# Prologue of a one-layer Hyena encoder: a new order of work, a shorter sine argument and transposes that nobody reads

## The chip, the cores and the metric

One NeuronCore of a Trainium2 chip runs the kernel. The metric is the device time of one execution in microseconds (us); less is better. The core has a matrix engine (PE), a vector engine (DVE), an activation engine (ACT), a general engine (POOL) and a synchronization engine (SP). Each works through its own queue in order. DMA transfers are started from the queues of SP, ACT and POOL and run beside the engines. PE writes only to PSUM, a small memory of eight banks; the other data lie in SBUF.

## What is computed

One Hyena layer followed by a SwiGLU channel mixer, on 1024 tokens of 1024 channels in float32. Cut to what matters here:

```python
def hyena_filter(L, w1, b1, w2, b2, w3, b3, freq, w_out, decay):
    ...
    act = lambda a: jnp.sin(fr * a)
    h = act(feat @ w1.astype(f32) + b1.astype(f32))
    h = act(h @ w2.astype(f32) + b2.astype(f32))
    h = act(h @ w3.astype(f32) + b3.astype(f32))
    h = (h @ w_out.astype(f32)).reshape(L, 2, D_MODEL)
    h = h * jnp.exp(-t[:, :, None] * jnp.abs(decay.astype(f32)))
    ...

def hyena_mixer(u, ...):
    z = short_conv(u @ w_in + b_in, conv_w, conv_b)      # width 3 along the tokens
    x0, x1, v = jnp.split(z, 3, axis=-1)
    s = (v * x1).astype(jnp.float32)
    g = hyena_filter(...)
    y = irfft(rfft(s, n=2L) * rfft(g, n=2L))[:, :L]
    y = (y + s * skip) * x0
    return y @ w_out + b_out

def reference(...):
    h = rmsnorm(x, norm_mix[i])
    x = x + hyena_mixer(h, ...)
    x = x + swiglu(rmsnorm(x, norm_ffn[i]), ...)
    return rmsnorm(x, norm_final)
```

The prologue is everything up to the first filter: the first RMS norm, its transposition, the first projections of `u @ w_in`, and the three sine layers of the filter.

## The kernel before, in words

**Numbers and tiles.** The 1024 tokens form 8 tiles of 128 (`xs[0..7]`), each with all 1024 channels. A float32 product is made from two parts of each operand: a high part, rounded to a shorter format, and a low part, the rest. Three of the four products of parts are summed (`TERMS`): high by high, high weight by low activation, low weight by high activation. One block of weights is `w_in[:, n*128:(n+1)*128]`; it gives `z{n}`, 128 channels by 1024 tokens, in two PSUM banks. Blocks 16 to 23 belong to `v`, 8 to 15 to `x1`, 0 to 7 to `x0`.

**Normalizing and turning.** For each tile ACT sums the squares (`square`, L269), ACT and DVE make the reciprocal root (`rstd`, L178 to L183), DVE multiplies by it and by the norm weight `gmix` (`scaled`, L280), PE transposes the tile with an identity matrix (`turn_in`, L285), ACT writes the high part (`u_high`, L292) and DVE the low part (`u_low`, L295). Tiles 4 and 5, and 6 and 7, share one `rstd`; tiles 0 to 3 have one each. `gmix` is loaded by SP with the same 4 KB row sent to all 128 partitions.

**Weights.** SP loads a block (`w_load`), ACT writes its high part (`w_high`, L199) and minus the high part into the place of the low part (L157), and a DMA of POOL's queue adds the raw block to that (L158). The raw tile can take the next block only after this DMA has landed.

**The sine layers.** PE multiplies (`mlp_mm`, L313), DVE adds the bias, multiplies by the frequency and takes off a multiple of two pi in eight passes of 512 elements (`mlp_angle`, L323 to L332), ACT takes the sine (`mlp_sin`, L335). After the third, `both_mm` (L340) and `hs_parts` (L346, L347) give the operand `hs` of the filter's product.

**The filter's window.** `F_[0].ready` and `F_[0].window(j)` take eight exponentials on ACT (L492). `taps` (L518, L519) multiplies the filter's product by them on DVE.

**The short convolution.** For `v` (`v_conv`) ACT makes the middle tap and both side taps, and two DMAs of POOL's queue add the side taps (L406, L416). For `x1` DVE adds them in four passes (`conv_rest`, L384, L385).

**Order.** The whole Hyena part is under a manual schedule: the order in which the program issues work is the order in each engine's queue, SP's and POOL's among them. After the prologue come eight periods, one for each 128 channels. A period begins with `taps_mm` (L511, L512), the first two steps of the next projection, and `spectrum_mm` (L528, L529). In the FFN behind, a planner sets the order of PE, DVE, ACT and POOL from estimated times.

**PSUM.** There are two slots of two banks with the tag `mm` and two with the tag `cv`. Before, all transposed tiles go through `cv`, and `mm` holds `z16` and `z8`. A slot is free again when the last reader or writer of its tile has finished.

Of the kernel before, what the change touches and what calls it, by code (L numbers as in the profile page):

```python
# [110 lines left out]
def hyena_ffn_kernel(ctx: ExitStack, tc: tile.TileContext, a: dict, out: bass.AP):  # L111
# [61 lines left out]
    S.sqrt(warm, ones)

    def rstd_of(ss, n, nm):
        w = small(nm, 4 * n, tag=f"rs{n}", bufs=2)
        sc, rt, r0, q = (w[:, i * n : (i + 1) * n] for i in range(4))
        V.tensor_scalar(sc, ss, 1.0 / D, EPS, ALU.mult, ALU.add)  # L178
        S.sqrt(rt, sc)
        V.reciprocal(r0, rt)  # L180
        V.scalar_tensor_tensor(q, sc, -0.5, r0, ALU.mult, ALU.mult)
        V.tensor_tensor(q, q, r0, ALU.mult)
        V.scalar_tensor_tensor(r0, q, 1.5, r0, ALU.add, ALU.mult)  # L183
        return r0

    c1, c2, c3 = _two_pi_parts()
# [9 lines left out]
    def w_high(n):  # L196
        whl = slot(f"whl{w_count[0] % 2}", f"whl{n}", (2, NB, P), F32R)
# [62 lines left out]
    load(xs[3], xv[:, 3, :])  # L260
    load(xs[4], xv[:, 4, :])
    w_load(8, "hs")
    for q in range(5, 8):
        load(xs[q], xv[:, q, :])

    xns, tps = {}, {}

    def square(j):
        S.activation(slot("sT", f"jk{j}"), xs[j], AF.Square, accum_out=sums[:, j : j + 1])  # L269

    rs = {}

    def rstd(j, n=1):
# [4 lines left out]
    def scaled(j):
        xn = xns[j] = slot(("s0", "s1", "xz", "vz")[j % 4], f"xn{j}")
        V.scalar_tensor_tensor(xn, xs[j], rs[j], gmix, ALU.mult, ALU.mult)  # L280

    def turn_in(j):
        pt = cv_psum(f"tp{j}")
        for k in range(NB):
            T.transpose(pt[:, k * P : (k + 1) * P], xns[j][:, k * P : (k + 1) * P], ident)  # L285
        tps[j] = pt.rearrange("p (k m) -> p k m", k=NB)
# [4 lines left out]
    def u_high(j):  # L291
        S.copy(u_of(0, j), tps[j])  # L292

    def u_low(j):
        V.tensor_tensor(u_of(1, j), tps[j], u_of(0, j).bitcast(F32), ALU.subtract)  # L295
# [12 lines left out]
    def half(t, li):  # L308
        return t[:, li // 2, li % 2 * 512 : (li % 2 + 1) * 512]

    def mlp_mm(li):
        pm = mlp_psum[li] = cv_psum(f"pmlp{li}")
        T.matmul(  # L313
            pm[:, 0:512],
            (w1, w2, w3)[li],
            feat if li == 0 else half(hnn, li - 1),
            start=True,
            stop=True,
        )

    def mlp_angle(li):
        ar, kq = half(ark, li), half(ark, 3)
        V.tensor_scalar(  # L323
            ar, mlp_psum[li][:, 0:512], cols2[:, li + 1 : li + 2], cols2[:, 0:1], ALU.add, ALU.mult
        )
        V.tensor_scalar(kq, ar, INV2PI, MAGIC, ALU.mult, ALU.add)
        V.tensor_scalar(kq, kq, MAGIC, None, ALU.subtract)
        yield 0
        for n, cc in enumerate((c1, c2, c3)):
            V.scalar_tensor_tensor(ar, kq, -cc, ar, ALU.mult, ALU.add)  # L330
            yield n + 1
        V.tensor_scalar(ar, ar, PI_IN, -PI_IN, ALU.min, ALU.max)  # L332

    def mlp_sin(li):
        S.activation(half(hnn, li), half(ark, li), AF.Sin)  # L335
# [13 lines left out]
    def piece(n, lo, hi, ti):  # L349
        if n not in z_psum:  # L350
            z_psum[n] = mm_psum(f"z{n}")
        wi, ui = TERMS[ti]
        for k in range(NB):
            T.matmul(
                z_psum[n][:, lo:hi],
                w_hl[n][wi][:, k, :],
                u2[ui][lo // 512][:, k, lo % 512 : (hi - 1) % 512 + 1],
                start=k == 0 and ti == 0 and lo % 512 == 0,
                stop=k == NB - 1,
                skip_group_check=ti > 0 or lo % 512 > 0,  # L360
            )
# [341 lines left out]
    w_high(8)
    piece(16, 0, 256, 1)
    u_high(3)
    square(4)
    square(5)
    run(angles[0], 1)
# [4 lines left out]
    piece(16, 256, 512, 0)
    piece(16, 256, 512, 1)
    rstd(4, 2)
    w_low(8)
    scaled(4)
    scaled(5)
    piece(8, 0, 512, 0)
    turn_in(4)  # L720
# [23 lines left out]
    F_[0].window(0)
    u_high(7)
    u_low(7)
    piece(8, 0, 512, 2)
    run(angles[1])
    for j in range(1, NB):
        F_[0].window(j)  # L750
    project(16, range(NB), (1,))
# [4 lines left out]
    w_split(17)
    w_load(0)
    run(angles[2])
    v_conv(0, lambda: mlp_sin(2))
    project(8, range(0, 6), (1,))  # L760
# [732 lines left out]
```

## Time and profile before

| what | us |
|---|---|
| median of three runs | 1198.18 |
| lowest and highest of them | 1196.16, 1200.47 |
| the profiled execution | 1202.94 |
| its span, first to last instruction | 1201.1 |
| PE busy, share of the span | 1162.7, 97% |
| DVE busy | 879.3, 73% |
| ACT busy | 520.6, 43% |

Rows of the timeline read: start, duration, engine, line, operation, output and inputs, shapes, how many instructions were merged, and in brackets the idle time before them with what ended it. "PEld" is PE's weight load, "SPq" and "POOLq" are issues of DMAs. Rows of the table by stretches read: busy time and number of instructions of each engine, then the granted clock of PE, the busy share of the DMA engines and what they moved.

### The profile page before, as it was taken

What the parts mean: (1) busy time and instruction counts of PE and PEld (TensorE: products, weight loads), DVE (VectorE), ACT (ScalarE), POOL (GpSimd) and SP (SyncE); (2) the same over time, 40 slices, a digit from 0 to 9 for tenths busy, and PEclk for the clock granted to TensorE, in tenths of its full rate; (3) what the DMA queues carried; (4) which work ended last, traced back from release to release, by engine and by line L of the source; (5) the groups of instructions that cost most, each with busy time, mean ns of one, the idle gap of its engine ahead of it and who ended that gap; (6) DMA issues with size and microseconds to landing.
All of it is one profiled execution on the core that took longest, in us unless ns stands there. A gap on an engine that the chain in (4) does not pass through costs nothing.

```text
span 1201.1 us, 15124 instructions
## 1 busy us (share of the span) xinstructions
PE 1162.7 (97%) x5694; PEld 968.2 (81%) x5694; DVE 879.3 (73%) x1426; ACT 520.6 (43%) x827; POOL 153.0 (13%) x218
## 2 busy tenths in 40 slices
PE   5899999999999999898999999999999989999997
PEld 4689898898988987776888888888888768888885
DVE  6788989889898894588747666566666458955675
ACT  6655544545445473465333322332333233334444
POOL 0001201112011140033101110011101100110000
PEclk9999999999999999999999999999999999999999
DMA  8546778777674799443313332233323359733323
GB/s 274 148 85 126 163 167 174 158 152 166 133 158 103 205 245 265 129 114 71 127 49 123 101 127 88 88 108 111 114 67 110 106 192 367 282 117 93 97 79 141
DMA packets 100998, 171.89 MB, mean 143 GB/s; under 512 B 7099, under 2 KB 60731, under 8 KB 100797
## 3 DMA queue, kind: packets, MB, share of 16 engines
q0 software_dynamic: 25120, 79.44, 28.8%
q1 hardware_dynamic: 75440, 91.11, 23.3%
q8 instruction: 45, 0.74, 0.2%
q10 hardware_dynamic: 365, 0.37, 0.1%
q14 instruction: 28, 0.23, 0.1%
HBM read 102.48 MB, written 40.11 MB: 119 GB/s over the span
## 4 chain that ended last, share of the span: by engine, by line
PE 51%; DVE 4%; DMA 2%; ACT 1%; issue 1%; SPq 0%; POOL 0%; POOLq 0%; DVEq 0%; ACTq 0%
PE bx L1366 9%; PE by L1366 5%; PE bz L1366 3%; PE po L864 1%; DMA hrp<-hd 1%; PE wu4dc L1122 1%; PE wg3dc L1122 1%; PE wg6dc L1122 1%; PE wg8dc L1122 1%; PE wu3dc L1122 1%; PE wu9dc L1122 1%; PE wg1dc L1122 1%; PE wu5dc L1122 1%; PE wg2dc L1122 1%; PE wg7dc L1122 1%
## 5 line engine op out<-in xcount | busy, mean ns | idle before, releaser
L148 PE MATMUL z<-uh,whl 128*128 128x512 f32 x736 | 206.7, 393 | 0.0
L148 PEld LDWEIGHTS z<-uh,whl 128*128 128x128 f32 x736 | 136.0, 188 | 27.3 <-issue 0.5
L1366 PE MATMUL bx<-wop,hop 128*128 128x512 f32 x480 | 114.0, 398 | 3.0 <-ACT hop L137 2.7
L148 PE MATMUL z<-ul,whl 128*128 128x512 f32 x368 | 115.1, 390 | 0.3 <-DVE ul L295 0.3
L1366 PEld LDWEIGHTS bx<-wop,hop 128*128 128x128 f32 x480 | 91.2, 190 | 24.7 <-ACT hop L137 3.1
L138 DVE TENSOR_TENSOR hop<-hrp,hop 128x1024 fp32r<-128x1024 f32 (+1 forms) x40 | 45.0, 1128 | 53.1 <-ACT hop L137 53.0
L137 ACT CAST hop<-hrp 128x1024 fp32r<-128x1024 f32 (+1 forms) x40 | 38.9, 974 | 99.8 <-PE bx L1366 43.4
L148 PEld LDWEIGHTS z<-ul,whl 128*128 128x128 f32 x368 | 69.1, 188 | 15.9 <-DVE ul L295 0.7
L864 PE MATMUL po<-wohl,uh 128*128 128x512 f32 x256 | 76.9, 402 | 1.6 <-DVE sig L657 1.4
L977 POOL DMA_DIRECT2D hd<-g x40 | 21.6, 543 | 328.0 <-DVE g L1282 191.4
L1366 PE MATMUL by<-wop,hop 128*128 128x512 f32 x264 | 61.1, 393 | 0.0
L864 PEld LDWEIGHTS po<-wohl,uh 128*128 128x128 f32 x256 | 48.1, 191 | 13.6 <-DVE sig L657 1.6
L1366 PEld LDWEIGHTS by<-wop,hop 128*128 128x128 f32 x264 | 49.7, 188 | 11.2
L199 ACT CAST whl<-wt 128x1024 fp32r<-128x1024 f32 x24 | 25.1, 1048 | 70.6 <-PE z L148 68.3
L138 DVE TENSOR_TENSOR wop<-wd,wop 128x512 fp32r<-128x512 f32 x73 | 47.5, 683 | 2.8 <-ACT wop L137 2.8
L529 PE MATMUL pg<-hw,fwd 128*128 128x128 f32 x256 | 49.5, 275 | 0.0
L528 PE MATMUL pg<-hw,fwd 128*128 128x128 f32 x256 | 49.5, 275 | 0.0
L137 ACT CAST wop<-wd 128x512 fp32r<-128x512 f32 x73 | 42.0, 616 | 15.5 <-PE by L1366 9.3
L158 POOL DMA_DIRECT2D whl<-wt x24 | 20.8, 865 | 219.0 <-ACT whl L157 116.3
L977 POOL DMA_DIRECT2D hrp<-hd x42 | 22.3, 531 | 192.7 <-DVE hop L138 162.7
L864 PE MATMUL po<-wohl,ul 128*128 128x512 f32 x128 | 45.3, 398 | 0.0
L528 PEld LDWEIGHTS pg<-hw,fwd 128*128 128x128 f32 x256 | 39.4, 192 | 0.6
(1573 smaller groups left out, 2817.7 us busy)
## 6 DMA issues: line engine op xcount, KB each, us to landing
hrp<-hd POOLq DMA_DIRECT2D x35, 512.0 KB, 4.0
wt<-in_hy_w_in_dram SPq DMA_DIRECT2D x24, 512.0 KB, 5.0
whl<-wt POOLq DMA_DIRECT2D x24, 512.0 KB, 4.8
wgr<-in_ffn_w_gate_dram SPq DMA_DIRECT2D x22, 512.0 KB, 3.9
wur<-in_ffn_w_up_dram SPq DMA_DIRECT2D x22, 512.0 KB, 4.2
wd<-in_ffn_w_down_dram SPq DMA_DIRECT2D x44, 256.0 KB, 6.8
hd<-g POOLq DMA_DIRECT2D x40, 256.0 KB, 2.6
hd<-sx POOLq DMA_DIRECT2D x30, 256.0 KB, 3.0
```

The costliest lines, as they stand in the source:

```text
L137: S.copy(hi, src)
L138: (eng or V).tensor_tensor(lo, src, hi.bitcast(F32), ALU.subtract)
L148: T.matmul(pt[:, h * 512 : (h + 1) * 512], w[wi], u2[ui][h][:, k, :], start=first and ti == 0, stop=last and ti == len(TERMS) - 1,)
L158: G.dma_start(lo.bitcast(F32), src, accum_op=ALU.add)
L199: S.copy(whl[:, 0], w_raw[n])
L528: T.matmul(o, fwd[r][:, j, :], f.hw[:, j, 0, :], start=True, stop=False)
L529: T.matmul(o, fwd[2 * r][:, jj, :], f.hw[:, jj, 1, :], start=False, stop=True)
L864: T.matmul(o, u2[yi][th][:, k, m * P : (m + 1) * P], wos[h][k // 2][wi][:, k % 2, :], start=(k == 0 and ti == 0), stop=(k == NB - 1 and ti ...
L977: G.dma_start(dst, src)
L1122: T.matmul(pt, t[:, wi, k, :], b(k)[ui], start=first and k == 0 and ti == 0, stop=k == 3 and ti == len(TERMS) - 1, skip_group_check=not first,
L1366: T.matmul(pt, ho[hi_][:, x, q * P : (q + 1) * P], wo_[wi][:, x, :], start=fresh and first and x == 0 and ti == 0, stop=last and x == n - ...
```

## The change

The change touches only what stands ahead of the first period.

- **Sine argument in turns.** DVE makes `(z + bias) * (freq / 2 pi)` in one pass (`mlp_turns`); two more passes round it and take the difference; ACT takes the sine with a scale of minus two pi. The eight passes become three.
- **rstd.** The mean and the epsilon go into ACT's operations (`scale`, `bias=epst`), and DVE has four small operations in place of five. Tiles 2 and 3 share one `rstd` too.
- **Norm weight.** One row of 4 KB is loaded (`rows`, ACT's queue); PE spreads it over 128 partitions with products by a row of ones (`spread_weight`), and DVE copies the two halves out of PSUM.
- **Loads.** The constants go through SP behind `xs[1]`; the tiles stand ahead of the weight blocks.
- **Projections by halves of tokens.** `first_half` and `second_half` make one term for 512 tokens, eight products of 512 columns; the order is written out anew.
- **Low parts of weights.** `w_low(16)` and `w_low(8)` are issued after `square(7)`. Block 17 takes the slot `cr`.
- **Convolution of block 0 of `v`** is made by `conv_rest` on DVE, not by DMAs.
- **Windows** of the first filter come after the last sine and after `conv_rest`.
- **Unread transposes.** `idle_products(n)` transposes the identity n times into a PSUM tile that nothing reads: 46 in all.
- `turn_in` of tiles 0 and 2 uses an `mm` slot.

```diff
+        rt, r0, q = (w[:, i * n : (i + 1) * n] for i in range(3))
+        S.activation(rt, ss, AF.Sqrt, bias=epst)
         V.reciprocal(r0, rt)
-        V.scalar_tensor_tensor(q, sc, -0.5, r0, ALU.mult, ALU.mult)
-        V.tensor_tensor(q, q, r0, ALU.mult)
+        V.scalar_tensor_tensor(q, ss, EPS, r0, ALU.add, ALU.mult)
+        V.scalar_tensor_tensor(q, q, -0.5, r0, ALU.mult, ALU.mult)
         V.scalar_tensor_tensor(r0, q, 1.5, r0, ALU.add, ALU.mult)
...
-    S.dma_start(cp, a["columns"])
-    S.dma_start(mc[0:66, 0:640], a["layer1"])
-    S.dma_start(mc[:, 640:896], a["layers"])
+    rows = slot("inv", "rows", (2, 1024))
+    S.dma_start(rows[0:1, 0], a["norm_mix"])
+    V.memset(rows[0:1, 1, 0:P], 1.0)
     load(xs[0], xv[:, 0, :])
-    load(gmix, a["norm_mix"].partition_broadcast(P)[:, 0, :])
     load(xs[1], xv[:, 1, :])
-    load(xs[2], xv[:, 2, :])
+    load(cp, a["columns"])
+    load(mc[0:66, 0:640], a["layer1"])
+    for q in range(2, 6):
+        load(xs[q], xv[:, q, :])
     w_load(16)
...
+    def idle_products(n):
+        for _ in range(n):
+            T.transpose(idle[:, 0:P], ident, ident)
+
+    def spread_weight():
+        pt = cv_psum("gain")
+        for h in range(2):
+            c = slice(h * 512, (h + 1) * 512)
+            T.matmul(pt[:, c], rows[0:1, 1, 0:P], rows[0:1, 0, c], start=True, stop=True)
+            V.tensor_scalar(gmix[:, c], pt[:, c], 1.0, None, ALU.mult)
...
+    def mlp_turns(li):
+        ar = half(ark, li)
+        V.tensor_scalar(ar, mlp_psum[li][:, 0:512], cols2[:, li + 1 : li + 2], turn, ALU.add, ALU.mult)
+
+    def mlp_sin(li):
         ar, kq = half(ark, li), half(ark, 3)
...
+        V.tensor_scalar(kq, ar, MAGIC, None, ALU.add)
+        V.scalar_tensor_tensor(ar, kq, MAGIC, ar, ALU.subtract, ALU.subtract)
+        S.activation(half(hnn, li), ar, AF.Sin, scale=-2.0 * PI_IN)
```

The new order, as it is issued:

```python
Filter(0); load(both, a["both"])
idle_products(10); spread_weight(); square(0); rstd(0); idle_products(6)
scaled(0); mlp_mm(0); idle_products(6); turn_in(0)
square(1); rstd(1); idle_products(6); scaled(1); square(2); square(3)
turn_in(1); turn = freq / 2 pi; mlp_turns(0); u_high(0)
rstd(2, 2); scaled(2); square(4); u_high(1); square(5); idle_products(12)
w_high(16); u_low(0); scaled(3); turn_in(2); u_low(1); rstd(4, 2); u_high(2)
turn_in(3); idle_products(6); scaled(4); u_high(3); turn_in(4); w_high(8)
u_low(2); scaled(5); u_low(3); square(6); square(7)
first_half(16, 0); w_low(16); first_half(8, 0); w_low(8); rstd(6, 2)
u_high(4); scaled(6); first_half(16, 1); turn_in(5); u_low(4); scaled(7)
first_half(8, 1); u_high(5); turn_in(6); u_low(5); u_high(6); turn_in(7)
u_low(6); u_high(7); mlp_sin(0); w_load(17); loads of fwd and inv
first_half(16, 2); u_low(7); second_half(16, 0); mlp_mm(1); F_[0].ready()
mlp_turns(1); w_high(17, "cr"); mlp_sin(1); w_low(17)
second_half(16, 1); second_half(16, 2); mlp_mm(2); w_load(0)
conv_params(); F_[0].low(); mlp_turns(2); conv_base(z0.vz, 16); mlp_sin(2)
second_half(8, 0); first_half(8, 2); both_mm(); hs_parts()
conv_rest(z0.vz, 16); F_[0].window(0) to F_[0].window(7)
second_half(8, 1); second_half(8, 2)
```

More of the change, by code (lines that the diff above doesn't have):

```diff
@@ L171, in hyena_ffn_kernel @@
     V.memset(ones, 1.0)
+    epst = small("epst", 1)
+    V.memset(epst, EPS)
     warm = small("warm", 1)
@@ L175, in rstd_of @@
     def rstd_of(ss, n, nm):
[L176 to L179, printed above, removed]
+        w = small(nm, 3 * n, tag=f"rs{n}", bufs=2)
+        rt, r0, q = (w[:, i * n : (i + 1) * n] for i in range(3))
+        S.activation(rt, ss, AF.Sqrt, bias=epst)
         V.reciprocal(r0, rt)
[L181 to L182 removed]
+        V.scalar_tensor_tensor(q, ss, EPS, r0, ALU.add, ALU.mult)
+        V.scalar_tensor_tensor(q, q, -0.5, r0, ALU.mult, ALU.mult)
         V.scalar_tensor_tensor(r0, q, 1.5, r0, ALU.add, ALU.mult)
         return r0
[L186 removed]
     w_raw, w_hl = {}, {}
@@ L194, in w_load, with w_high @@
         w_raw[n] = wt
-    def w_high(n):
-        whl = slot(f"whl{w_count[0] % 2}", f"whl{n}", (2, NB, P), F32R)
+    def w_high(n, tag=None):
+        whl = slot(tag or f"whl{w_count[0] % 2}", f"whl{n}", (2, NB, P), F32R)
         w_count[0] += 1
@@ L319, in mlp_mm @@
         )
-    def mlp_angle(li):
-        ar, kq = half(ark, li), half(ark, 3)
[L323 to L335, printed above, removed]
+    turn = small("turn", 1)
+    def mlp_turns(li):
+        ar = half(ark, li)
+        V.tensor_scalar(ar, mlp_psum[li][:, 0:512], cols2[:, li + 1 : li + 2], turn, ALU.add, ALU.mult)
+    def mlp_sin(li):
+        ar, kq = half(ark, li), half(ark, 3)
+        V.tensor_scalar(kq, ar, MAGIC, None, ALU.add)
+        V.scalar_tensor_tensor(ar, kq, MAGIC, ar, ALU.subtract, ALU.subtract)
+        S.activation(half(hnn, li), ar, AF.Sin, scale=-2.0 * PI_IN)
     def both_mm():
@@ L671, in add_bias, with first_half, second_half @@
         G.dma_start(xb[:, j], a["hy_b_out"].partition_broadcast(P)[:, 0, :], accum_op=ALU.add)
+    def first_half(n, ti):
+        piece(n, 0, 512, ti)
+    def second_half(n, ti):
+        if n not in z_psum:
+            z_psum[n] = mm_psum(f"z{n}")
+        wi, ui = TERMS[ti]
+        for k in range(NB):
+            T.matmul(
+                z_psum[n][:, 512:1024],
+                w_hl[n][wi][:, k, :],
+                u2[ui][1][:, k, :],
+                start=k == 0 and ti == 0,
+                stop=k == NB - 1 and ti == len(TERMS) - 1,
+            )
@@ L673, in hyena_ffn_kernel @@
     Filter(0)
     load(both, a["both"])
-    mlp_mm(0)
-    angles = [mlp_angle(li) for li in range(3)]
+    idle_products(10)
+    spread_weight()
     square(0)
     rstd(0)
+    idle_products(6)
     scaled(0)
-    run(angles[0], 0)
+    mlp_mm(0)
+    idle_products(6)
+    turn_in(0)
     square(1)
-    turn_in(0)
     rstd(1)
+    idle_products(6)
     scaled(1)
+    square(2)
+    square(3)
+    turn_in(1)
+    V.tensor_scalar(turn, cols2[:, 0:1], INV2PI, None, ALU.mult)
+    mlp_turns(0)
@@ L685, in hyena_ffn_kernel @@
     u_high(0)
-    square(2)
-    rstd(2)
+    rstd(2, 2)
     scaled(2)
-    turn_in(1)
+    square(4)
+    u_high(1)
+    square(5)
+    idle_products(12)
     w_high(16)
-    square(3)
-    u_high(1)
     u_low(0)
-    rstd(3)
     scaled(3)
     turn_in(2)
-    w_low(16)
+    u_low(1)
+    rstd(4, 2)
     u_high(2)
-    u_low(1)
-    piece(16, 0, 256, 0)
     turn_in(3)
-    u_low(2)
[L703 to L708, printed above, removed]
@@ L709, in hyena_ffn_kernel @@
-    run(angles[0], 2)
-    run(angles[0], 3)
-    run(angles[0])
-    u_low(3)
[L713 to L720, printed above, removed]
+    idle_products(6)
+    scaled(4)
+    u_high(3)
+    turn_in(4)
+    w_high(8)
+    u_low(2)
+    scaled(5)
+    u_low(3)
     square(6)
     square(7)
+    first_half(16, 0)
+    w_low(16)
+    first_half(8, 0)
+    w_low(8)
+    rstd(6, 2)
     u_high(4)
-    rstd(6, 2)
+    scaled(6)
@@ L725, in hyena_ffn_kernel @@
+    first_half(16, 1)
+    turn_in(5)
     u_low(4)
-    scaled(6)
-    turn_in(5)
+    scaled(7)
+    first_half(8, 1)
     u_high(5)
-    piece(8, 0, 512, 1)
-    mlp_sin(0)
+    turn_in(6)
     u_low(5)
-    scaled(7)
-    turn_in(6)
-    mlp_mm(1)
     u_high(6)
-    piece(16, 0, 512, 2)
     turn_in(7)
     u_low(6)
+    u_high(7)
+    mlp_sin(0)
     w_load(17)
@@ L741, in hyena_ffn_kernel @@
         load(fwd[i], a["fwd"][:, i])
+    inv = slot("inv", "inv", (2, NB, P))
     load(inv, a["inv"])
+    first_half(16, 2)
+    u_low(7)
+    second_half(16, 0)
+    mlp_mm(1)
     F_[0].ready()
[L744 to L751, printed above, removed]
+    mlp_turns(1)
+    w_high(17, "cr")
     mlp_sin(1)
+    w_low(17)
+    second_half(16, 1)
+    second_half(16, 2)
     mlp_mm(2)
+    w_load(0)
     conv_params()
     F_[0].low()
[L756 to L760, printed above, removed]
+    mlp_turns(2)
+    z0 = blocks[0]
+    z0.vz = slot("vz", "vz0")
+    conv_base(z0.vz, 16)
+    mlp_sin(2)
+    second_half(8, 0)
+    first_half(8, 2)
     hs = slot("hs", "hs", dt=F32R)
@@ L763, in hyena_ffn_kernel @@
     hs_parts()
-    project(8, range(6, 8), (1,))
-    second_tap(16)
+    conv_rest(z0.vz, 16)
+    F_[0].window(0)
+    F_[0].window(1)
+    F_[0].window(2)
+    F_[0].window(3)
+    F_[0].window(4)
+    F_[0].window(5)
+    F_[0].window(6)
+    F_[0].window(7)
+    second_half(8, 1)
+    second_half(8, 2)
     def period(b):
```

21 lines of the change are left out of this document (8 added, 13 removed).

## The prediction

> **What bounds the kernel now.** I read the table of busy times by stretches first, then the waits of PE, then the timeline of the first 70 us.
>
> ```profile
> 0.00:20.00 20.00, 9.36 (x34) 6.88 (x34) 11.99 (x30) 11.81 (x20) 1.74 (x7) 1.00 0.93 312
> 20.00:38.00 18.00, 14.68 (x92) 12.08 (x91) 14.54 (x24) 14.50 (x22) 0.86 (x1) 1.00 0.89 249
> 38.00:60.00 22.00, 20.53 (x90) 15.14 (x89) 15.17 (x28) 14.31 (x23) 2.54 (x3) 1.00 0.44 88
> 60.00:110.00 50.00, 50.00 (x296) 44.11 (x295) 44.84 (x76) 24.97 (x38) 5.98 (x7) 1.00 0.56 115
> ```
>
> The columns are PE, PE's weight loads, DVE, ACT, POOL, granted clock, DMA share, GB/s. From 60 to 110 us PE is busy all the time. Before 60 us no engine is: PE works 9.36 of the first 20 us, 14.68 of the next 18, 20.53 of the next 22. So the prologue is bound by a chain that crosses the engines, and the rest by PE.
>
> ```profile
> PE po L864 <- DVE sig L657: 1.4, 1, 1.4
> ```
>
> ```profile
> 55.47 0.38 PE L511 MATMUL ph<-fwh,hs 128*128 128x256 f32 x1
> ...
> 56.82 0.19 PEld L511 LDWEIGHTS ph<-fwh,hs 128*128 128x128 f32 x1 [0.35 <-DVE hs L347]
> ...
> 60.63 0.38 PE L528 MATMUL pg<-hw,fwd 128*128 128x128 f32 x2
> ```
>
> The first is the longest wait of PE between 57 and 490 us, 1.4; the others are of the timeline. So I take the first product of `spectrum_mm`, at 60.63, as the mark: behind it the order of PE is the same, and what the mark gains, the kernel gains.
>
> **The change part by part.** The change reorders everything ahead of the mark, so the cost is not a sum of edits: it is the new chain, from durations of the old rows. The reduced edits count only where they lie on it.
>
> ```profile
> 1.02 0.29 POOL masks.py:199 TENSOR_SCALAR_AFFINE_SELECT ident<-ident 128x128 f32<-128x128 f32 x1
> ...
> 4.99 1.06 ACT L269 ACTIVATE jk<-xt 128x1024 f32<-128x1024 f32 x1 [2.31 <-DMA xt<-in_x_dram]
> 5.95 0.19 ACT L269 ACTIVATION_READ_ACCUMULATOR jk<-xt 128x1 f32 x1
> ...
> 6.35 0.20 ACT L179 ACTIVATE ra<-ra 128x1 f32<-128x1 f32 x1 [0.22 <-DVE ra L178]
> 6.59 0.16 DVE L180 RECIPROCAL ra<-ra 128x1 f32<-128x1 f32 x1 [0.27 <-ACT ra L179]
> ...
> 7.17 0.16 DVE L183 SCALAR_TENSOR_TENSOR ra<-ra 128x1 f32<-128x1 f32 x1
> 7.44 1.28 DVE L280 SCALAR_TENSOR_TENSOR xn<-xt,ra,gmix 128x1024 f32<-128x1024 f32 x1
> 8.64 0.81 DVE L323 TENSOR_SCALAR ark<-pmlp,cp 128x512 f32<-128x512 f32 x1
> ...
> 15.34 1.22 DVE L295 TENSOR_TENSOR ul<-tp,uh 128x1024 fp32r<-128x1024 f32 x1
> 16.76 1.04 ACT L157 ACTIVATE whl<-whl 128x1024 fp32r<-128x1024 f32 x1
> 34.38 1.01 ACT L292 CAST uh<-tp 128x1024 fp32r<-128x1024 f32 x1 [1.51 <-PE tp L285]
> 65.08 0.69 DVE L466 TENSOR_TENSOR g0ab<-pg,g0ab 128x512 f32<-128x512 f32 x1 [1.07 <-ACT g0ab L465]
> ```
>
> A square with its read costs 1.15. From L180 to L183 three steps take 0.58, so the four small DVE operations of an `rstd` take 0.8.
>
> ```profile
> 6.37 2.08 PE L313 MATMUL pmlp<-mc 66*128 66x512 f32 x2 [6.37 <-DMA mc<-in_layer_dram]
> 8.87 1.94 PE L285 MATMUL tp<-ident,xn 128*128 128x128 f32 x8 [0.42 <-DVE xn L280]
> ...
> 16.62 1.97 PE L285 MATMUL tp<-ident,xn 128*128 128x128 f32 x8 [1.60 <-DVE ra L178]
> 18.24 1.84 PE L354 MATMUL z<-uh,whl 128*128 128x256 f32 x8
> 20.14 1.10 PE L285 MATMUL tp<-ident,xn 128*128 128x128 f32 x8
> 25.98 2.01 PE L354 MATMUL z<-uh,whl 128*128 128x512 f32 x8
> 27.83 1.91 PE L285 MATMUL tp<-ident,xn 128*128 128x128 f32 x16
> 34.37 1.10 PE L313 MATMUL pmlp<-hnn,mc 128*128 128x512 f32 x2
> ```
>
> PE starts slow: eight transposes take 1.97 at 16.62 and 1.10 at 20.14, one layer's product 2.08 and later 1.10, though the granted clock reads 1.00 throughout. The speed doubled near 20 us, after PE had run from 16.62 without a gap. A warm half (eight products of 512) takes 1.85, from 25.98 to 27.83; a warm sine product adds 0.9 to a queue, since its tail overlaps.
>
> *A, the norm weight.* The identity is there at 1.31. Ten slow transposes (0.24 each) end at 3.8. The two spreading products, 2.08 slow and 1.10 warm by the rows of the same width, end near 7.2 if PE speeds up between them, at 8.0 if not. The copy of 512 values out of PSUM is priced by L466 at 0.69: `gmix` is there at 7.9. In the old trace it didn't delay `scaled(0)` at 7.44, so this part begins with a loss. The 4 KB row must land by 3.8. Nothing shows such a small load; the nearest row is the first one of the same queue:
>
> ```profile
> cp<-in_columns_dram ACTq DMA_DIRECT2D x1, 70.0 KB, 4.5
> ```
>
> From its issue at 0.74 that is 5.2 at most, a loss of 1.4 more. I take "by 3.8", since the old load was 17 times larger and shared the engines with three big ones, and keep 1.4 for the range. [...]
>
> *B, DVE from 7.9.* `rstd(0)`, `scaled(0)`, `rstd(1)`, `scaled(1)`, `turn` (0.16, as L180) and `mlp_turns(0)` (0.81), `rstd(2,2)`, `scaled(2)`, `u_low(0)`, `scaled(3)`: 3 x 0.8 + 4 x 1.28 + 0.97 + 1.22 = 9.7, to 17.6. ACT and a warm PE lie beside it: `turn_in(0)` needs `xn0` at 10.0 and ends at 11.2, `u_high(0)` at 12.2, ahead of the root for tiles 2 and 3.
>
> *C, ACT.* `turn_in(3)` ends at 18.7. Then `u_high(3)` 1.01, `w_high(8)` 1.04, two squares 2.30, both low activations of the weights 2.08, the root for tiles 6 and 7 0.20: 6.6, to 25.3. DVE has done up to `u_low(3)` by 24.6 and waits here for the first time. Block 8 must land by 19.7:
>
> ```profile
> 10.00:20.00 10.00, 6.16 (x28) 5.22 (x26) 8.64 (x21) 8.29 (x15) 1.03 (x1) 1.00 1.07 366
> ```
>
> Behind `xs[0]`, which had landed when L269 began at 4.99, 4.96 MB stand up to the end of block 8; at 366 GB/s that is 18.5. The broadcast of the norm weight, 0.52 MB, is gone from this queue.
>
> *D, DVE.* `rstd(6,2)`, `scaled(6)`, `u_low(4)`, `scaled(7)`, `u_low(5)`: 0.8 + 2 x 1.28 + 2 x 1.22 = 5.8, to 31.1. `turn_in(7)` needs the PSUM slot that `u_low(5)` frees, and ends at 32.2. PE itself, with its four first halves and two transpositions behind `turn_in(4)`, would be there at about 31.5.
>
> *E, PE without a gap.* Six halves (11.1), two sine products (1.8), `both_mm` with twice the columns of one (2.0 with its tail): to 47.1. Each sine hides beside halves: DVE's turns (0.81) and two passes of at most 0.81 each plus ACT's sine stand beside 3.7 us of halves, with some 0.7 us to spare. If they are slower, this cover goes first.
>
> *F, the end.*
>
> ```profile
> 39.15 2.91 ACT L492 ACTIVATE hw<-dc,cp 128x256 f32<-128x256 f32 x7
> ...
> 54.10 0.59 ACT L346 CAST hs<-pboth 128x512 fp32r<-128x512 f32 x1 [0.84 <-PE pboth L340]
> 54.72 0.69 DVE L347 TENSOR_TENSOR hs<-pboth,hs 64x512 fp32r<-64x512 f32 x1 [3.36 <-ACT hs L346]
> ...
> 56.80 2.50 DVE L518 TENSOR_TENSOR hw<-ph,hw 128x1024 f32<-128x1024 f32 x2
> ...
> 59.35 2.85 DVE L384 SCALAR_TENSOR_TENSOR xz<-z,cp,xz 128x896 f32<-128x896 f32 x4
> ...
> 30.94 1.28 ACT L335 ACT_TABLE_LOAD   x1
> ```
>
> `hs_parts` takes two copies and two differences, 2.6; `conv_rest` 2.85; the taps 2.50; two small operations like L180, 0.3: 8.3, so the mark can start at 55.4. ACT's window beside it (a table load of 1.28 and eight exponentials, 3.3, after the second copy at 49.0) ends at 53.6, before the second half of the taps at 54.0. PE needs two halves (3.7) and what stood between 55.47 and 60.63 (4.8 without its wait of 0.35): 55.6. So DVE, ACT and PE come out nearly level, and I take 55.6. What the edits drop (POOL's side taps, ACT's two extra table loads, five passes per sine) shortens only queues beside this chain.
>
> The chain has some twelve hand-offs between engines, 0.03 to 0.15 each in the rows above; with 0.6 for them the mark stands at 56.2. **Sum:** 60.6 - 56.2 = 4.4 us earlier. The profiled execution took 1202.94, its span 1201.1; they become 1198.5 and 1196.7. It lay 4.8 above the median, so on the median's scale: 1198.2 - 4.4 = 1193.8. With the bounds of A and the hand-offs this case alone reaches from 1192.3 to 1196.0.
>
> **The rivals.** *PE stays slow (the other side).* The unread transposes may not wake the clock. Between 7.2 and 18.7 PE's list holds 30 unread transposes, one sine product and four tiles; warm this is about 8.5 us of work, slow 17. If the speed changes at time t, the list ends near 12.1 + t/2: it costs from t = 13, and the gain is gone at t = 22. Slow to its end it puts `turn_in(3)` at 24.1 in place of 18.7: the gain of 4.4 becomes a loss of 1.0, 1199.2. Against it: the old switch near 20.1 followed 3.5 unbroken us of which 1.6 were transposes. For it: from 6.37 to 10.8 PE was nearly unbroken too, half of it transposes, and stayed slow. [...]
>
> *Block 17 arrives late.* Its load waits for the raw tile of block 16, whose low part is now issued after both last squares, near 24.1.
>
> ```profile
> DMA to landing us min/median/max: 4.6/6.7/10.4
> ...
> DMA to landing us min/median/max: 4.5/5.8/10.4
> ```
>
> The first row is the low parts' DMA, the last the loads of blocks. In medians block 17 lands at 24.1 + 6.7 + 5.8 = 36.6; it may be 38.7 before `w_high(17)` holds up the second sine on ACT. At both highest values it lands at 44.9, 6.2 late: 1200.0. The loads of `fwd` and `inv` stand behind it in SP's queue, but have 10 us more.
>
> *The planner turns.* The FFN's order on PE is planned, and its last part has gaps:
>
> ```profile
> 945.00:990.00 45.00, 39.95 (x165) 31.75 (x164) 22.91 (x30) 14.85 (x22) 5.34 (x10) 0.95 0.57 187
> 990.00:1201.00 211.00, 202.82 (x873) 164.72 (x872) 144.12 (x246) 90.31 (x155) 18.59 (x35) 0.99 0.49 167
> ```
>
> PE idles 5.1 and 8.2 us there. A changed start can move such gaps by a few us either way: 1190 to 1198. A uniform shift should leave the plan alone, which speaks against it.
>
> **How the numbers follow.** Forecast 0.60, slow PE 0.18, block 17 late 0.08, planner 0.14. A measurement of this kernel can tell about 0.3%, 3.6 us: faster means below 1194.6. Two thirds of the forecast's own range lie below it, and about half of the planner's: faster 0.49, same 0.45, slower 0.06. The range from 1190.5 to 1199.3 takes in slow PE and most of the planner's and block 17's cases.
>
> **What would show it.** Right: `scaled(0)` starts near 8.7; transposes take about 1.1 from `turn_in(0)` on; the root for tiles 6 and 7 near 25.3; PE unbroken from 32 us; the mark near 56.2; no new waits of PE behind it. Wrong: transposes of 1.9 behind 13 us; `w_high(17)` waiting for a DMA; PE waiting for a sine; a mark that gains and a span that doesn't.

## The result: the mark came earlier, the kernel later

| kernel | median us | lowest to highest | ratio to before [95% interval] | mark |
|---|---|---|---|---|
| before, measured beside it | 1198.7 | 1196.16 to 1200.47 | 1 | 60.63 |
| after | 1207.57 | 1206.03 to 1208.48 | 1.0074 [1.0055, 1.0092] | 56.95 |

The changed kernel is 8.9 us slower, outside the predicted range. (Here and below, medians and ranges leave out single runs at a far lower granted clock: one of after, 1665.99 us at 0.656, one of `a_few`, 1663.86 at 0.655, and one of before, 1950.76 at 0.56.) Yet its prologue did nearly what was forecast: the mark, the first product of `spectrum_mm`, stands 3.7 us earlier. The profiled execution took 1206.03, its span 1204.2.

The table of busy times by stretches of after, with the columns PE, PE's weight loads, DVE, ACT, POOL, granted clock, DMA share, GB/s:

```profile
0.00:20.00 20.00, 16.04 (x76) 11.03 (x77) 11.18 (x25) 12.73 (x22) 0.71 (x6) 1.00 0.92 301
20.00:38.00 18.00, 16.55 (x93) 13.69 (x91) 14.52 (x21) 13.47 (x19) 1.94 (x2) 1.00 0.62 161
38.00:60.00 22.00, 21.76 (x111) 17.44 (x110) 15.31 (x29) 10.62 (x17) 0.85 (x1) 1.00 0.36 109
60.00:110.00 50.00, 50.00 (x294) 43.55 (x293) 44.44 (x73) 26.09 (x40) 5.96 (x7) 1.00 0.51 111
```

PE is fuller ahead of 60 us: 54.4 us of the first 60 where before had 44.6. From 60 to 110 both kernels keep PE busy without a gap, but after does 294 products there and before did 296. Two products of some 230 ns are about 0.5 us. The reader who looks only at busy shares sees nothing here; the loss is in the count beside them.

The timeline says the same with more leverage. First rows of `spectrum_mm` in the first, second and eighth period, before (its first row stands in the prediction) and then after:

```profile
106.89 0.38 PE L528 MATMUL pg<-hw,fwd 128*128 128x128 f32 x2
...
407.33 0.38 PE L528 MATMUL pg<-hw,fwd 128*128 128x128 f32 x2
```

```profile
56.95 0.38 PE L530 MATMUL pg<-hw,fwd 128*128 128x128 f32 x2
...
103.92 0.38 PE L530 MATMUL pg<-hw,fwd 128*128 128x128 f32 x2
...
408.24 0.38 PE L530 MATMUL pg<-hw,fwd 128*128 128x128 f32 x2
```

From the second mark to the eighth before takes 300.44 us, after 304.32: 50.07 and 50.72 a period. The lead of 3.7 us shrinks by 0.71 us in the first period and by 0.65 in each of the next six, and is a lag of 0.9 at the eighth mark. A loss that is the same in each period, with PE hardly ever idle, is unlikely to be a wait. Something that PE does is longer.

Groups by line and form of PE, both kernels, from 60 to 460 us (busy us, then mean ns of one):

```profile
L148 PE MATMUL z<-uh,whl 128*128 128x512 f32 x698 | 193.8, 392 | 0.0
```

```profile
L140 PE MATMUL z<-uh,whl 128*128 128x512 f32 x696 | 196.7, 397 | 0.0
```

The product of the projections, the same operation on the same shapes, takes 397 ns in place of 392. Products overlap, so the mean of one isn't its price. From start to start, between the second mark and the eighth, it is 232.3 ns in after and 227.5 in before. That is 4.8 ns on each of 144 products in a period, or 0.69 us, about the 0.65 that is lost. The 128-wide products of the spectrum (`pg`) have a mean of 275 ns in both kernels. The FFN shows it as well. Products in a stretch in which PE is never idle, before and then after:

```profile
575.00:940.00 365.00, 365.00 (x1589) 297.89 (x1588) 232.85 (x338) 110.57 (x170) 34.02 (x63) 1.00 0.30 99
```

```profile
575.00:940.00 365.00, 365.00 (x1573) 295.32 (x1573) 231.46 (x335) 109.57 (x169) 34.11 (x63) 1.00 0.29 99
```

365 us by 1589 is 229.7 ns a product, by 1573 it is 232.0. The granted clock is 1.00 in both. So the question for the experiments: why does a product that nobody edited, hundreds of microseconds behind the edit, take 1 to 2% longer?

### The profile page after: what moved, and what is told of

It reads as the page before. It is cut to its first block, busy times and chain, and to the rows that moved or that the text cites. A ratio compares the mean times of both kernels' runs of the same rounds, so it can differ in the third digit from the quotient of the medians.

```text
span 1204.2 us, 15168 instructions
## 1 busy us (share of the span) xinstructions
PE 1178.9 (98%) x5728; PEld 973.1 (81%) x5728; DVE 876.2 (73%) x1414; ACT 516.1 (43%) x818; POOL 151.6 (13%) x216
## 4 chain that ended last, share of the span: by engine, by line
PE 51%; DVE 3%; DMA 2%; ACT 1%; issue 1%; POOL 0%; SPq 0%; ACTq 0%; POOLq 0%
PE bx L1397 9%; PE by L1397 5%; PE bz L1397 3%; PE wg0dc L1153 1%; DMA hrp<-hd 1%; PE po L895 1%; PE wg1dc L1153 1%; PE wu8dc L1153 1%; PE wu5dc L1153 1%; PE wu3dc L1153 1%; PE wg6dc L1153 1%; PE wu7dc L1153 1%; PE wu2dc L1153 1%; PE wu9dc L1153 1%; PE wg5dc L1153 1%
## 5 line engine op out<-in xcount | busy, mean ns | idle before, releaser
L140 PE MATMUL z<-uh,whl 128*128 128x512 f32 x704 | 199.1, 398 | 0.2 <-DVE vz L386 0.2
L140 PEld LDWEIGHTS z<-uh,whl 128*128 128x128 f32 x704 | 130.4, 189 | 28.7 <-PE ph L514 0.4
L140 PE MATMUL z<-ul,whl 128*128 128x512 f32 x352 | 110.1, 394 | 0.0
L140 PEld LDWEIGHTS z<-ul,whl 128*128 128x128 f32 x352 | 66.3, 188 | 15.6
L895 PEld LDWEIGHTS po<-wohl,uh 128*128 128x128 f32 x256 | 48.1, 191 | 13.9 <-DVE sig L659 2.0
```

The lines of the kernel that those rows point to most:

```text
L140: T.matmul(pt[:, h * 512 : (h + 1) * 512], w[wi], u2[ui][h][:, k, :], start=first and ti == 0, stop=last and ti == len(TERMS) - 1,)
L895: T.matmul(o, u2[yi][th][:, k, m * P : (m + 1) * P], wos[h][k // 2][wi][:, k % 2, :], start=(k == 0 and ti == 0), stop=(k == NB - 1 and ti ...
```

## The experiments

What the edit changes for those products is where their operands lie. In SBUF the change adds two tiles of 4 bytes a partition (`epst`, `turn`), takes the slots of one tag earlier, and moves `inv` (its slot now holds `rows` first). In the compiled kernels the high parts of the weights start at 195200 and 207488 bytes before, at 195328 and 207616 after: 128 bytes further. Modulo 256 bytes, most other tiles move by 32 or 64; the activations stay at 16512. In PSUM the two tags trade places: `mm` has banks 4 to 7 before and 0 to 3 after. **The theory** is SBUF: the weights' new addresses slow the products. **The rival** is PSUM: the other banks do. A third is that the unread transposes leave PE or its clock in another state.

### The moved addresses alone: b_sbuf and b_psum

`b_sbuf` is the kernel before with the SBUF addresses of after, and nothing else of the change; the new tiles are there and idle.

```diff
+    epst = small("epst", 1)
+    V.memset(epst, EPS)
...
-    inv = slot("inv", "inv", (2, NB, P))
...
+    inv = slot("inv", "inv", (2, NB, P))
...
+    turn = small("turn", 1)
+    V.memset(turn, 1.0)
...
+    V.memset(small("pad", 8, tag="rs2", bufs=2), 1.0)
```

> The kernel before with the SBUF addresses of the changed kernel: small unused tiles move the weight tiles by 128 bytes and the constants by 32, and the slot of the inverse constants lies behind the token tiles; the order of work is the old one. Theory A (the products run slower because the stationary tiles lie elsewhere against the moving ones): 512-wide products of the projections take 231 ns from start to start in place of 227, a period 50.7 in place of 50.07, the time about 1206 to 1209. Theory B (the PSUM banks) and theory C (the new order of work itself): 227 ns, 50.07, about 1199.

`b_psum` is the kernel before with one unread transpose ahead of the first sine layer, which turns the order of the two tags in PSUM.

```diff
+    first = mm_psum("first")
+    T.transpose(first[:, 0:P], ident, ident)
```

> The kernel before with one unread transpose ahead that takes the first PSUM slot, so that the projections' sums lie in banks 0 to 3 and the other slots in 4 to 7, as in the changed kernel; SBUF as before. Theory B (the banks): 231 ns per product, 50.7 per period, about 1206 to 1209. Theories A and C: 227 ns, 50.07, about 1199.

`b_sbuf` took 1208.61 us (1205.27 to 1210.61), 1.0073 [1.0056, 1.0089] times before, which had 1198.97 beside it. `b_psum` took 1197.77 (1194.44 to 1202.84), 0.9986 [0.9969, 1.0003]. The group of the projections' products, 60 to 460 us, in `b_sbuf` and the stretch of the FFN, then the group in `b_psum`:

```profile
L148 PE MATMUL z<-uh,whl 128*128 128x512 f32 x698 | 197.2, 397 | 0.0
```

```profile
575.00:940.00 365.00, 364.96 (x1572) 294.98 (x1571) 233.00 (x338) 110.16 (x169) 34.74 (x64) 1.00 0.30 100
```

```profile
L148 PE MATMUL z<-uh,whl 128*128 128x512 f32 x700 | 194.4, 392 | 0.0
```

Moving some tiles makes the old kernel 9.6 us slower by the medians, with the mean of after, 397, and nearly its count, 1572. Its mark hardly moves (60.73). The banks show no effect. The size fits: from the first mark to the eighth `b_sbuf` loses 4.6 us, and 17 products fewer in 365 us, at 232 ns, are 3.9; together 8.5 of the 9.6. Where the rest is lost wasn't told apart.

### The change without the moved addresses: a_sbuf

After with the addresses of before: the small tiles share one allocation, two shared `rstd` use the tag of the single ones, and the slot of `rows` is taken where `inv` was.

```diff
-    ones = small("ones", 1)
+    few = small("ones", 3)
+    ones, epst, turn = (few[:, i : i + 1] for i in range(3))
...
+    rows = slot("inv", "rows", (2, 1024))
...
-    rstd(2, 2)
+    rstd(2, 2, "rs1")
```

> The changed kernel with the SBUF addresses of the kernel before (its small tiles share one, the slot of the inverse constants is taken first); order of work and PSUM banks as changed. Theory A: 227 ns, 50.07 per period, and the gain of 3.7 us at the first product of the first filter spectrum stays to the end: about 1195. Theories B and C: 231 ns, 50.7, about 1208.

It took 1196.72 us (1192.95 to 1198.63), 0.9978 [0.9966, 0.9989] times before. The group and the stretch of the FFN:

```profile
L140 PE MATMUL z<-uh,whl 128*128 128x512 f32 x696 | 193.2, 392 | 0.0
```

```profile
575.00:940.00 365.00, 365.00 (x1589) 297.95 (x1588) 234.88 (x340) 109.72 (x172) 35.19 (x65) 1.00 0.29 98
```

392 and 1589 are back, and the median is 10.9 us below that of after. The whole reordering, 46 unread transposes included, stands in both kernels, so it isn't what slows the products. At the addresses of before the change is a small gain: 2.25 us by the medians, with the mark at 57.53, 3.1 earlier. Of the 3.7 that were to stay to the end, not all did.

### Fewer unread transposes: a_few

After, with one unread transpose at each of its six places in place of 46 in all.

```diff
-        for _ in range(n):
+        for _ in range(1):
```

> The changed kernel with one unread transpose at each of the six places in place of 46 in all. Theory D (the unread transposes wake the clock): the clock comes some us after 12.2, and the first spectrum product, at 56.95, moves later by 0.5 to 4. Rival (the transposes are not needed, the spreading products and the first layer wake it): it moves by under 0.3 or comes earlier. Either way the products behind stay at 231 ns.

It took 1204.85 (1199.62 to 1209.44), 1.0043 [1.0025, 1.006] times before: still slower, and its products still start 232.3 ns apart. So the transposes aren't the cause of the loss. But the mark came at 56.23, 0.7 earlier than with 46. What they do to the clock is in the timeline and the table by stretches, of `a_few`:

```profile
2.55 2.04 PE L267 MATMUL gain<-rows 1*128 1x512 f32 x2 [0.71 <-DMA rows<-in_norm_mix_dram]
...
12.18 1.90 PE L291 MATMUL tp<-ident,xn 128*128 128x128 f32 x8
...
16.71 3.17 PE L291 MATMUL tp<-ident,xn 128*128 128x128 f32 x16 [2.52 <-DVE ul L301]
```

```profile
13.90:17.20 3.30, 0.78 (x7) 0.54 (x6) 3.23 (x5) 3.30 (x6) 0.00 (x0) 1.00 1.06 359
17.30:20.60 3.30, 2.80 (x14) 2.27 (x12) 3.16 (x7) 1.92 (x4) 0.00 (x0) 0.50 0.72 170
```

The same in after:

```profile
12.20:15.50 3.30, 3.30 (x33) 3.30 (x32) 2.53 (x7) 1.90 (x3) 0.00 (x0) 1.00 1.09 379
17.30:20.60 3.30, 2.39 (x20) 2.16 (x21) 3.27 (x5) 2.82 (x6) 0.00 (x0) 1.00 0.76 178
```

In both the full clock is there by 14 us (12.2 in after, where eight transposes take 1.04 us at 12.53; 13.9 in `a_few`, where one takes 0.42 at 11.96 and 0.27 at 13.92). In `a_few` PE then works 0.78 of 3.30 us, and the next stretch reads 0.50. In after all of the 33 instructions from 12.2 to 15.5 are transposes, read and unread, and the clock reads 1.00 there and from 17.3 to 20.6. So here the clock stayed at 1.00 with transposes alone. The other profiles agree: with 46 unread transposes (after, `a_sbuf` and `a_align46` below) none reads a half clock in the prologue (`a_align46` has 1.00 from 12 to 21 us), and with six (`a_few`, and `a_align`, `a_off128` and `a_bcast` below) each reads one, of 3.4 or 6.8 us (`a_align` has 0.50 from 16.1 to 19.3, after PE was busy for 0.71 of 3.20 us). Whether transposes alone would raise the clock isn't shown, since products stand among those ahead of 12 us. The transposes also stand in PE's queue, and in both pairs that differ in them alone (here, and `a_align46` against `a_align`) the mark comes later with 46, by 0.7 and 1.9 us.

### The disputed quantity by itself: micro

This kernel computes nothing of the reference. PE runs 20 groups of 64 products of 128x512, and beside the second ten no other engine works. The moving tile is one and the same, and the stationary tiles `wk` to `wt` start 0, 32, 64, 96, 128, 160, 192, 224, 256 and 512 bytes behind it modulo 512 (`wa` to `wj` are a first round of the same).

```python
OFFSETS = (0, 32, 64, 96, 128, 160, 192, 224, 256, 512)
...
for i, w in enumerate(ws):
    for r in range(8):
        for k in range(8):
            nc.tensor.matmul(pt, w[:, k, :], mv[:, k, :], ...)
```

> Nothing of the reference is computed: one core runs 20 groups of 64 products of 128 by 512 in the short float format, the moving tile always the same and starting at 128 modulo 256, the stationary tiles starting 0, 32, 64, 96, 128, 160, 192, 224, 256 and 512 bytes further modulo 512 (wa to wj, then again wk to wt); no other engine works beside them. Theory A1 (what counts is the distance of the two starts modulo 256): 227 to 228 ns per product for 0, 256 and 512, 231 or more for the others. Theory A2 (what counts is the start of the stationary tile alone): the fast ones need not be those three. Theory A3 (the delay comes from other engines that use SBUF beside PE): all ten alike.

Groups by form of the second round, in the order of the offsets (busy us of 64 products, then the mean of one):

```profile
L50 PE MATMUL pt<-mv,wk 128*128 128x512 f32 x64 | 14.7, 389 | 0.0
...
L50 PE MATMUL pt<-mv,wl 128*128 128x512 f32 x64 | 15.1, 395 | 0.0
...
L50 PE MATMUL pt<-mv,wo 128*128 128x512 f32 x64 | 15.0, 395 | 0.0
...
L50 PE MATMUL pt<-mv,wq 128*128 128x512 f32 x64 | 14.8, 392 | 0.0
...
L50 PE MATMUL pt<-mv,ws 128*128 128x512 f32 x64 | 14.7, 389 | 0.0
L50 PE MATMUL pt<-mv,wt 128*128 128x512 f32 x64 | 14.7, 389 | 0.0
```

From start to start in the second round. The first round agrees within 0.1, but for its first group, which began before the full clock was granted (the mean granted clock of the run is 0.985):

| distance, bytes | 0 | 32 | 64 | 96 | 128 | 160 | 192 | 224 | 256 | 512 |
|---|---|---|---|---|---|---|---|---|---|---|
| ns a product | 226.7 | 233.3 | 233.4 | 234.1 | 232.4 | 233.3 | 229.1 | 233.3 | 226.7 | 226.7 |

A busy time of 14.7 us less the last product's 389 ns, over 63 steps, is 227 ns; 15.1 less 395 gives 233. So the time of a product changes with the start of its stationary tile: 226.7 ns where it lies at 0 modulo 256 bytes from the moving one, 229.1 to 234.1 at the others tried (231 or more had been expected of all of these; 192 bytes gave 229.1). The moving tile never moves here, so this kernel alone can't tell the distance of the two from the address of the stationary one; `a_off128` below does. Before has its weights at 128 modulo 256, where the activations are as well: 227.5. After has them at 0: 128 bytes apart, and 232.3, which is the 232.4 of the small kernel. The FFN's products at 229.7 ns say that the kernel before was slow there already: in its program many of them have their operands 64 or 192 bytes apart.

### All tiles at one distance: a_align and a_off128

`a_align` is `a_few` with 32 floats of padding and the small tiles ahead of the large ones, so that every large tile starts at 128 modulo 256, as the activations do. `a_off128` has 64 floats: all large tiles are then 128 bytes from the activations.

```diff
+PAD = 32
...
+    turn = small("turn", 1)
+    for n in (1, 2):
+        V.memset(small(f"pad{n}", 8, tag=f"rs{n}", bufs=2), 1.0)
+    V.memset(small("pad", PAD), 1.0)
...
-    turn = small("turn", 1)
```

> The changed kernel with all large tiles at 128 modulo 256, as the activations are, and with one unread transpose at each of the six places. Theory A1: the projections at 227 ns as in the kernel before, and the FFN's products, of which some had their weights at 64 modulo 256 in the kernel before, faster too: mean below 229.0 against 230.0 in the FFN and below 230.0 against 230.6 behind it; the time 1190 to 1195, under that of the kernel before. Theory A2: somewhere between 1196 and 1207.

> The same kernel as the aligned one with 128 bytes more of padding: all large tiles at 0 modulo 256, the activations still at 128. Theory A1: 231 ns in the projections and 232 in the FFN for products with the activations as moving operand, though every tile lies on a round address; the time 1202 to 1208. Rival (round addresses are the fast ones): as fast as the aligned one.

`a_align` took 1185.39 us (1184.85 to 1185.4), 0.9891 [0.9877, 0.9904] times before; it beats both kernels, and lies 4.6 us below the lowest time expected of it. `a_off128` took 1197.56 (1193.61 to 1202.77), 1.0 [0.9984, 1.0016]. Stretch of the FFN and group of the projections, first `a_align`, then `a_off128`, and last a group of the FFN's down-projection in `a_off128`:

```profile
575.00:940.00 365.00, 365.00 (x1612) 302.21 (x1611) 237.08 (x343) 111.72 (x173) 37.79 (x71) 1.00 0.30 101
```

```profile
L141 PE MATMUL z<-uh,whl 128*128 128x512 f32 x696 | 193.1, 392 | 0.0
```

```profile
575.00:940.00 365.00, 365.00 (x1583) 296.95 (x1582) 232.31 (x336) 110.09 (x170) 34.01 (x63) 1.00 0.29 99
```

```profile
L141 PE MATMUL z<-uh,whl 128*128 128x512 f32 x696 | 196.4, 397 | 0.0
```

```profile
L1400 PE MATMUL by<-wop,hop 128*128 128x512 f32 x264 | 60.2, 389 | 0.0
```

1612 products in the stretch are 226.4 ns each, the fast value of the small kernel; 1583 are 230.6. Padding that differs by 128 bytes is worth 12.2 us. `a_off128` came out 4 us below the lowest time expected of it: I had counted the down-projection of the FFN among the slow products, but both of its operands lie among the moved tiles, at distance 0; their mean is 389 ns and they start 226.7 to 226.8 ns apart. The FFN's gate and up products agree: those whose two operands both moved start 228.0 ns apart, those that read the activations 233.0. So in this run tiles at 0 modulo 256 are fast together, at 226.7 to 228.0 ns, and slow with the activations at 128, at 233.0: the time goes with the distance between the operands, not with the address of either.

### The new order against the old one at equal distances: b_align and a_align46

`b_align` is before with the same alignment (48 floats of padding); `a_align46` is `a_align` with all 46 unread transposes, which is after with nothing but its tiles moved. The second excerpt shows its edit against `a_align`.

```diff
+PAD = 48
...
+    for n in (1, 2):
+        V.memset(small(f"pad{n}", 8, tag=f"rs{n}", bufs=2), 1.0)
+    V.memset(small("pad", PAD), 1.0)
```

```diff
-        for _ in range(1):
+        for _ in range(n):
```

> The kernel before, its order of work untouched, with all large tiles at 128 modulo 256. By the distance rule the FFN's products fall from 230.0 to about 226.7 ns and those behind from 230.6 to 226.5, as in the aligned version of the changed kernel: 1600 x 3.3 + 870 x 4.1 ns = 8.9 us, so 1189 to 1190. Then the new order of work is worth the rest of the aligned version's gain, 4 to 5 us. If instead the aligned version's gain came from its order, this kernel stays at 1194 or above.

> The aligned version with all 46 unread transposes, that is the changed kernel with nothing but its large tiles moved. The unread transposes cost: the first spectrum product at 56.7 as in the changed kernel, in place of 55.8 with six, the time 1186 to 1187. They pay: 55.8 or earlier, and no return of the clock to half before 20 us.

`b_align`: 1189.13 us (1184.95 to 1190.59), 0.9909 [0.9882, 0.9936]. `a_align46`: 1187.14 (1185.92 to 1189.88), 0.9899 [0.9872, 0.9927]. The marks, in the order `b_align`, `a_align46`, `a_align`:

```profile
61.38 0.38 PE L532 MATMUL pg<-hw,fwd 128*128 128x128 f32 x2
```

```profile
57.88 0.38 PE L533 MATMUL pg<-hw,fwd 128*128 128x128 f32 x2
```

```profile
55.98 0.38 PE L533 MATMUL pg<-hw,fwd 128*128 128x128 f32 x2
```

At equal distances the new order puts the mark 3.5 us earlier, and with six unread transposes 5.4. By the medians 2.0 and 3.7 of that reach the end, where 4 to 5 had been expected; the 3.7 compares two sets of runs, in which before differed by 1.4. The intervals overlap, so neither is more than the measurement can tell; that `a_sbuf` gained 2.25 with an interval below 1 supports the 2.0. The 40 transposes that `a_align` leaves out cost 1.9 us at the mark; at the end the medians differ by 1.75, which these runs can't tell from nothing. The marks are of one execution each, and one order doesn't always give one mark: 56.95, 57.53 and 57.88 for the order of after, 60.63 to 61.38 for that of before. Differences at the mark below some 0.9 us are within that.

### The norm weight by a broadcast load: a_bcast

`a_align` with the old load of the norm weight, the same row to all partitions, right behind `xs[0]`, and no spreading products.

```diff
-    S.dma_start(rows[0:1, 0], a["norm_mix"])
...
     load(xs[0], xv[:, 0, :])
+    load(gmix, a["norm_mix"].partition_broadcast(P)[:, 0, :])
     load(xs[1], xv[:, 1, :])
...
-    spread_weight()
```

> The aligned kernel with the norm weight loaded for all partitions by a transfer, as before, right behind the first tile, in place of the spreading products. Theory E (the spreading products hold up the first scaled tile and with it the chain): scaled(0) from about 8 to 7.5 us, the first spectrum product earlier by 0.5 to 2, the time the same or up to 2 us less. Rival (the 0.5 MB ahead of the other tiles hold up the chain as long): the first spectrum product at the same place or later by up to 2 us.

It took 1187.6 us (1185.64 to 1188.75), 0.9911 [0.9896, 0.9926], 2.2 more than `a_align`, with the mark at 58.83, 2.9 later. Timeline of `a_align`, then of `a_bcast`:

```profile
5.97 1.06 ACT L278 ACTIVATE jk<-xt 128x1024 f32<-128x1024 f32 x1
...
8.64 1.28 DVE L291 SCALAR_TENSOR_TENSOR xn<-xt,ra,gmix 128x1024 f32<-128x1024 f32 x1
```

```profile
7.52 1.28 DVE L291 SCALAR_TENSOR_TENSOR xn<-xt,ra,gmix 128x1024 f32<-128x1024 f32 x1
8.47 1.06 ACT L278 ACTIVATE jk<-xt 128x1024 f32<-128x1024 f32 x1 [1.77 <-DMA xt<-in_x_dram]
```

So the rival had the direction, though it allowed 2 at most. Without the spreading `scaled(0)` starts 1.1 us earlier, where 0.5 had been expected. But the load stands ahead of `xs[1]`, whose square starts 2.5 later. The lead on the first tile is used up by that: `scaled(1)` starts at 10.77 against 10.62, and `scaled(2)` 1.8 later, at 15.83. PE's clock also read 0.50 for 6.8 us in this prologue and for 3.4 in that of `a_align`, so how much of the 2.9 each of the two made isn't told apart.

## Why the prediction was wrong

The step that failed is the one that carries the mark to the end: "behind it the order of PE is the same, and what the mark gains, the kernel gains". The order is the same; the duration is not. The products behind the mark went from 227.5 to 232.3 ns in the projections and from 229.7 to 232.0 in the FFN, because the change shifted their stationary tiles against their moving ones. `b_sbuf` shows that this shift alone costs 9.6 us, `a_sbuf` that without it 10.9 come back, and the small kernel shows the dependence with nothing else running. No rival of the prediction had it; its list of signs names "a mark that gains and a span that doesn't", without a cause. The tiles' addresses are in no row of the profile; what could have raised the question is in the change: it adds small tiles and moves a slot, and so everything allocated behind them.

At the distances of before, the forecast would have had its sign, and not its full size: `a_sbuf` stands at 0.9978, a gain of 2.25 us where 4.4 was forecast. Step by step, with the chain of after from its timeline:

```profile
3.70 2.07 PE L267 MATMUL gain<-rows 1*128 1x512 f32 x2
...
6.55 2.07 PE L267 MATMUL gain<-rows 1*128 1x512 f32 x2 [0.78 <-DVE gmix L268]
...
8.66 0.69 DVE L268 TENSOR_SCALAR gmix<-gain 128x512 f32<-128x512 f32 x1 [2.16 <-PE gain L267]
...
10.04 1.28 DVE L286 SCALAR_TENSOR_TENSOR xn<-xt,ra,gmix 128x1024 f32<-128x1024 f32 x1
...
12.53 1.04 PE L291 MATMUL tp<-ident,xn 128*128 128x128 f32 x8
...
17.97 1.27 DVE L286 SCALAR_TENSOR_TENSOR xn<-xt,ra,gmix 128x1024 f32<-128x1024 f32 x1
...
26.43 0.28 ACT L172 ACTIVATE ra<-sums,epst 128x2 f32<-128x2 f32 x1
31.11 1.23 DVE L301 TENSOR_TENSOR ul<-tp,uh 128x1024 fp32r<-128x1024 f32 x1
37.31 1.03 ACT L190 CAST whl<-wt 128x1024 fp32r<-128x1024 f32 x1
46.34 1.88 PE L342 MATMUL pboth<-hnn,both 128*128 128x512 f32 x4
```

| step | predicted | measured |
|---|---|---|
| A, `gmix` ready | 7.9 | 9.35 |
| `scaled(0)` starts | 8.7 | 10.04 |
| B, `scaled(3)` ends | 17.6 | 19.24 |
| C, root of tiles 6 and 7 ends | 25.3 | 26.71 |
| D, `u_low(5)` ends | 31.1 | 32.34 |
| E, `both_mm` ends | 47.1 | 48.2 |
| the mark | 56.2 | 56.95 |

- **A was mis-sized by 1.45 us.** I let the two spreading products run back to back, the second at the warm price. Both write one PSUM tile, and the second waited 0.78 for the copy of the first half; both took the slow 2.07. The row itself was no limit: in after the product began at 3.70 without a wait on the load, and in `a_few`, where fewer transposes stand ahead of it, it waited until 2.55, 1.8 us after the load's issue at 0.74.
- **B to F were right in size.** The delay of A is handed down, 1.6, 1.4, 1.2, 1.1, and 0.75 are left at the mark. At the end of the prologue ACT's last exponential ends at 54.8, DVE's taps at 56.4, and PE reaches the mark at 56.95: nearly level, as F had it.
- **Slow PE** did not come true. Eight transposes take 1.04 at 12.53: the speed changed near 12.2, ahead of the 13 from which this rival costs anything. The row of after from 12.20 to 15.50, transposes alone at a clock of 1.00, against the 0.50 that `a_few` reads from 17.30 to 20.60 with six unread ones, speaks against it too, as far as keeping the clock goes.
- **Block 17** did not wait: `w_high(17)` at 37.31 has no wait on a DMA.
- **The planner** did not turn PE's order: behind the mark the programs of before and after have the same 4960 products of PE in the same order. Its idle time from 945 us on is no larger: in after PE is busy for 42.44 us from 945 to 990 and 204.85 from 990 to 1201, more than the prediction's rows of before show.
- **The passes of the sine argument** were miscounted: before has seven on DVE, not eight, so four fall away and not five. They lie on no step of the chain, as the prediction had it.

What stays open: at equal distances the mark gains 3.1 to 3.5 us and the end 2.0 to 2.25. In the profiled executions of `b_align` and `a_align46` the lead is still 3.9 at the end of the last products of `inv` (466.0 against 462.1), 2.4 at the first product of the FFN and 1.2 at the end of its last product ahead of the down-projection. Between these points PE has idle times. One execution of each doesn't tell a cause from scatter.

## What to carry to other kernels

Here two more tiles of 4 bytes and a moved slot shifted the weights by 128 bytes and cost 9.6 us. So when a change adds, drops or moves an SBUF tile, and a time moves and no wait does, compare the mean of the products that nobody edited, and the number of products in a stretch in which PE is never idle. If these have changed, look at the distance between the starts of stationary and moving tile modulo 256 bytes before looking at the edit, and pad until it is 0 (226.7 ns a product here, against 229.1 to 234.1 at the other distances): that was worth more than the whole reordering (10 us on the kernel before, 20 on the one after). A working by a chain of steps gave the prologue to 0.8 us; it failed because it took the price of everything behind the chain as fixed.

## What the runs showed beside

- In `micro`, products of 128x512 in the shorter format start 226.7 ns apart when both operands start at the same address modulo 256 bytes, and 229.1 to 234.1 at the seven other distances tried. Why the distance counts, the runs don't show.
- How often PE's clock reads 0.50 differs between executions that have the same order of PE behind the mark. The profiled execution of before reads it three times between the prologue and its last product, for 3.4 us each, after PE had been busy for 0.90, 1.43 and 0.73 of the 3.40 us ahead; that of `a_few` reads it nowhere there. Before, then `a_few`:

```profile
497.60:500.90 3.30, 3.30 (x10) 2.65 (x9) 2.04 (x8) 2.74 (x5) 0.00 (x0) 0.50 0.21 79
...
961.80:965.10 3.30, 2.99 (x7) 2.44 (x8) 2.70 (x5) 3.30 (x6) 0.34 (x1) 0.50 0.41 153
...
989.10:992.40 3.30, 3.30 (x10) 2.46 (x9) 3.30 (x5) 1.46 (x3) 0.53 (x1) 0.50 0.39 61
```

```profile
490.00:570.00 80.00, 73.98 (x344) 58.18 (x343) 64.99 (x124) 43.27 (x83) 21.86 (x19) 1.00 0.38 96
...
945.00:990.00 45.00, 42.60 (x182) 33.56 (x181) 26.52 (x35) 15.87 (x23) 6.50 (x13) 1.00 0.61 196
```

  In each of these stretches of before PE does 7 to 10 products in 3.30 us where some 14 fit at 230 ns, by estimate a loss of 1 to 1.6 us. That may be part of the scatter between executions: in `a_few` the mean granted clock goes from 0.997 in the fastest run, 1199.62 us, to 0.992 in the slowest, 1209.44. It is a reason to compare medians of many runs rather than two profiles.
